# Accumulators of the backward gate's first block in the shared PSUM banks, and splits of attention values at the highest priority

## The chip, the cores and the metric

The kernel runs on one core of a Trainium2 chip. The metric is the device time of one execution in microseconds; lower is better. The kernel before takes 435.74 us, the median of three runs (435.19 to 435.88).

## The reference

One inference step of a hybrid diffusion backbone with one layer. 128 context tokens and 512 latent tokens (a grid of 8 rows of 64) of width 1024 go through the same weights. Each token is normalised, scaled and shifted by a modulation vector, and multiplied by one input projection of 1024 x 3840. Its columns feed three branches: neighbourhood attention with 8 heads of 64 (a query sees a window of 8 x 16 grid positions and 256 cached context keys), a gated linear recurrence in both directions with 4 heads and a 64 x 64 state each, and a Fourier transform over positions. Each branch is multiplied by a SiLU gate, and one output projection, a normalisation and a residual follow. Cut to what matters here:

```python
h = _rmsnorm(x, g_pre) * (1 + scale) + shift
proj = h @ w_in
qa, ka, va, ga, qr, zf, zb, ir, gr, uf, gf = _split_columns(proj)
...
lf_f, k_f = _hgrn_gates(zf, lb_f)      # forward gate of the recurrence
lf_b, k_b = _hgrn_gates(zb, lb_b)      # backward gate
...
s = jnp.concatenate([s_lat.reshape(B, H, GRID_W, kh * GRID_W), s_ctx], axis=-1)
p = jax.nn.softmax(s, axis=-1).astype(v.dtype)
v_all = jnp.concatenate([v_r.reshape(B, kh * GRID_W, H, dh), v_ctx], axis=1)
return jnp.einsum('bhqk,bkhd->bqhd', p, v_all)
```

## The kernel before

**Precision and splits.** Every operand of a large product is held as a high and a low part of a reduced format. `split` (L129 to L131) makes them: ScalarE casts the source to the high part (L130), VectorE subtracts it from the source to get the low part (L131). A product of two such operands is three matmuls (`mm3`, L210). All matmuls are recorded at the helper's line L113 and all transposes at L127; both run on TensorE.

**Blocks.** The input projection is cut into 30 blocks of 128 columns (the list `BLOCKS`). `block` (L299) loads one block's weights, splits them, and goes over the 640 tokens in two halves of 320 (u = 0 and 1). Each half is summed in one PSUM accumulator by 8 steps of three matmuls, 24 in all, and is then handed to a function that reads the accumulator. The modulated input, transposed, lies in `hT` as high and low part.

**PSUM banks.** There are eight banks. `PB(tag)` (L105) takes one from one of two pools by its tag: "b" has five banks, "f" has three (`WB`, L27). A bank that is asked for is waited for until the instructions that read its last contents are done. Pool "f" holds mostly the blocks' accumulators; pool "b" serves the start stage, the recurrence's levels and states, the attention's scores, transposes and sums.

**Start.** For each of the eight 128-row steps k of the input, `start_stream` (L244) computes the modulation, transposes the scaled input (`modulated`, L233, two "b" banks per step) and writes step k of `hT`. The forward gate's two blocks (zf0, zf1) are summed alongside in four accumulators, three of pool "f" and one of pool "b" (L208). When the last step is in, `gate` (L321) reads each with two sigmoids on ScalarE (L325, L326).

**Order of the work.** Generators for the start, the recurrences, the attentions and the blocks are interleaved by a small planner (`Order`, L39) with estimated costs and delays. The order in which it traces instructions is their priority. From it the program builder makes the final order of each engine's instructions: it simulates the engines, and on each one takes the ready instruction of the highest priority. A tile's buffer or bank is also given out in this simulation. `tc.high_priority()` puts the instructions traced inside it ahead of all others that are ready. On the chip each engine then works through its own list in order. `FILL` (L30) names the order of blocks: zb0 qr0 zb1 qr1 ir0 P0 P1 ga0 P2 and so on. zb0 is the backward gate's first block; P0 to P3 are the four attention pairs (two heads each).

**An attention pair.** `attention_blocks` (L574) runs block va (values), starts block qa (queries), and after two of its steps turns the values back to token order: `by_token` (L343) transposes the five blocks of 128 tokens, the first four into one "b" bank and the fifth into an "f" bank of its own. For each of the two heads three splits follow (L630 to L632): four token blocks from the "b" bank (128x256), one from the "f" bank (128x64), and the two blocks of cached values, which come from SBUF (`vcf`, tile `cf`). Their results lie in the tile `vs`. Then the cached keys are split, and blocks qa and ka go on. `attention` (L638) computes scores, softmax (L677 to L685), transposes of the probabilities and the weighted sums.

**The recurrence.** Each of its two parts goes through seven levels (L453 to L478) with six VectorE products, four ScalarE copies and masked copies out of PSUM (L451), then states (L504 to L528), whose recursion is L525, and outputs (L530 to L545).

Of the kernel before, what the change touches and what calls it, by code (L numbers as in the profile page):

```python
# [71 lines left out]
def mixer_kernel(ctx: ExitStack, tc: tile.TileContext, A, O):  # L72
# [14 lines left out]
    def nm(s):  # L87
        n_[0] += 1
        return f"{s}_{n_[0]}"

    def T(cols=NT, dt=F32, tag=""):
        return tp.tile([P, NT], dt, tag="t", name=nm("t" + tag))[:, :cols]
# [9 lines left out]
    def C():  # L102
        return sp.tile([P, 256], F32, tag="cf", name=nm("cf"), bufs=WB["cf"])

    def PB(tag="b"):  # L105
        return ps.tile([P, 512], F32, tag=tag, name=nm("pb"), bufs=WB["p" + tag])
# [22 lines left out]
    def split(src, hi, lo, hi_eng=None, lo_eng=None):  # L129
        (sc.copy if hi_eng is None else hi_eng.tensor_copy)(hi, src)  # L130
        (ve if lo_eng is None else lo_eng).tensor_sub(lo, src, hi.bitcast(F32))  # L131
# [16 lines left out]
    RS = [slice(0, 64), slice(64, 128)]  # L148
# [37 lines left out]
    def load_w(src, lo_eng=None, shape=(KT, P), tags=("raw", "hi", "lo")):  # L186

        return split_w(load_raw(src, tags[0], shape), lo_eng, shape, tags[1:])

    def load(t, src):  # L190

        with tc.issue_after(wdma[-1]) if wdma else ExitStack():
            sy.dma_start(t, src)
# [16 lines left out]
    def mm3(out, w, k, u, first, last):  # L210

        for a, (ww, hh) in enumerate(((w[0], 0), (w[0], 1), (w[1], 0))):
            mm(out, ww[:, k, :], hT[hh][:, k, 320 * u:320 * u + 320], start=(first and a == 0), stop=(last and a == 2))
# [85 lines left out]
    def block(name, use, lo_eng=ve):  # L299

        w = load_w(A["win"][BLOCKS.index(name)], lo_eng)
        for u in range(2):
            acc = PB("bf"[u] if name == "zb0" else "f")[:, 0:320]
            for k in range(KT):
                if name == "zb0" and u == 0 and f"h{k}" not in od.events:
                    yield f"h{k}"
                mm3(acc, w, k, u, k == 0, k == KT - 1)
                if k % 2 and k < KT - 1:
                    yield 0
            use(acc, u)  # L310
            if u == 1:
                od.set(f"block{nb[0]}", 0.0)
                nb[0] += 1
            yield 0
# [28 lines left out]
    def by_token(src):  # L343

        pt = PB(), PB("f")
        for i in range(5):
            tr(pt[i // 4][:, i % 4 * P:i % 4 * P + P], src[:, i * P:(i + 1) * P])
        return [(slice(4 * j, 4 + j), pt[j][:, 0:(4, 1)[j] * P].rearrange("p (i e) -> p i e", e=P)) for j in range(2)]
# [208 lines left out]
    def gate_block(name):  # L557
        j = GATE[name[:2]] + int(name[2])

        g = T(tag="g")  # L560

        def use(z, u):
            twice_silu(g[:, HF[u]], z)
            if u == 0:
                return
            if j in (4, 5):
                ve.tensor_scalar(g, g, late["ghg"][:, j - 4:j - 3], 0.5, op0=ALU.mult, op1=ALU.mult)
            mixed(j, gate=g)
        yield from block(name, use)
# [4 lines left out]
    def attention_blocks(p):  # L574
        tbl = sp.tile([P, 2, 2, 256], F32, tag="tbl", name=nm("tbl"), bufs=WB["tbl"])
        kf, kcf = T(tag="k"), C()
        vcf = C().rearrange("p (j e) -> p j e", e=P)
        load(kcf, A["kc"][p])
        load(vcf, A["vc"][:, :, p * P:(p + 1) * P])
        load(tbl, A["tbl"][p])  # L580
        vT, q = T(), T(tag="q")


        qs = [T(tag="qs", dt=F32R) for _ in range(2)]
        ks = [T(tag="ks", dt=F32R) for _ in range(2)]
        kcs = [sp.tile([P, 256], F32R, tag="kc", name=nm("kc"), bufs=WB["kc"]) for _ in range(2)]
        vs = tp.tile([P, 2, 7, P], F32R, tag="vs", name=nm("vs"), bufs=WB["vs"])
        att[p] = (tbl, qs, ks, kcs, vs)

        RW = slice(0, 3), slice(3, 8)  # L590

        def latent(z, u):
            return z[:, P * (1 - u):].rearrange("p (r c) -> p r c", c=64)

        def use_v(z, u):
            if u == 0:
                sc.copy(vT[:, 0:P], z[:, 0:P])
                sy.dma_start(O["o_v"][p], vT[:, 0:P])
            sc.copy(vT[:, P:NT].rearrange("p (j r c) -> p j r c", j=4, c=16)[:, :, RW[u], :],
                    latent(z, u).rearrange("p r (j c) -> p j r c", c=16))  # L600

        def use_q(z, u):
            if u == 0:
                sc.mul(q[:, 0:P], z[:, 0:P], 0.125)
            zl = latent(z, u)
            ql = q[:, P:NT].rearrange("p (q r c) -> p q r c", q=4, c=16)[:, :, RW[u], :]
            sc.mul(ql[:, 0:3], zl[:, :, 8:56].rearrange("p r (j c) -> p j r c", j=3), 0.125)
            sc.mul(ql[:, 3, :, 0:8], zl[:, :, 56:64], 0.125)
            sc.mul(ql[:, 3, :, 8:16], zl[:, :, 0:8], 0.125)
            if u == 0:  # L610
                return
            split(q, *qs, ve, QE)

        def use_k(z, u):
            if u == 0:
                ve.tensor_copy(kf[:, 0:P], z[:, 0:P])
                sy.dma_start(O["o_k"][p], kf[:, 0:P])
            ve.tensor_copy(kf[:, P:NT].rearrange("p (j r c) -> p j r c", j=4, c=16)[:, :, RW[u], :],
                           latent(z, u).rearrange("p r (j c) -> p j r c", c=16))
            if u == 0:  # L620
                return
            split(kf, *ks, ve, KE)
            od.set(f"a{p}", LAT["prep"])

        yield from block(f"va{p}", use_v)
        q_gen = block(f"qa{p}", use_q)
        yield next(q_gen)
        yield next(q_gen)
        vp = by_token(vT)
        for hh in range(2):  # L630
            for sl, src in vp + [(slice(5, 7), vcf)]:
                split(src[:, :, RS[hh]], vs[:, hh, sl, RS[hh]], vs[:, hh, sl, RS[1 - hh]])  # L632
        split(kcf, *kcs, ve, CE)
        yield 0
        yield from q_gen
        yield from block(f"ka{p}", use_k)
# [321 lines left out]
    def fill():  # L958
        yield "h4"
        for step in FILL.split():  # L960
            if step == "|":
                yield 0
                continue
            n, p = step[:2], int(step[-1])
            if n == "zb":
                yield from block(step, lambda z, u: gate(p, 1, z, u), ve)
            elif n == "qr":
                yield from block(step, lambda z, u: query(p, z, u), ve)
            elif n == "ir":
                yield from value_blocks()  # L970
            elif n[0] == "P":
                yield from attention_blocks(p)
            elif n[0] == "m":
                yield step
            elif n == "uf":
                yield from fourier_blocks()
            elif n == "F0":
                od.streams.insert(0, [fourier(), od.now])
            else:
                yield from gate_block(step)  # L980
        yield from out_first()
        yield from out_second()
# [148 lines left out]
```

## Time and profile before

| | before |
|---|---|
| median of three runs | 435.74 us |
| profiled execution | 436.31 us |
| its span, first to last instruction | 434.5 us |
| TensorE matmuls, busy | 410.3 us (94%) |
| TensorE weight loads, busy | 373.0 us (86%) |
| VectorE, busy | 303.2 us (70%) |
| ScalarE, busy | 204.7 us (47%) |
| DMA, mean of 16 engines | 110 GB/s |

PE is TensorE's matmul, PEld its weight load, which overlaps it, DVE VectorE, ACT ScalarE, POOL GpSimd and SP the engine that issues the DMAs. A row of a timeline gives start, duration, engine, line, operation, output and inputs, shape and count; in brackets stands how long the engine had idled before it, and what it had waited for. Where several like instructions follow each other, one row stands for all, with the time from the first start to the last end.

### The profile page before, as it was taken

How to read it: one execution, taken by the hardware profiler on the slowest of the kernel's cores; microseconds unless marked ns; L12 is line 12 of the kernel's file. 1: busy time of each engine (PE TensorE's matmuls, PEld its weight loads, DVE VectorE, ACT ScalarE, POOL GpSimd, SP SyncE). 2: the span in 40 equal slices, each digit the busy share in tenths (PEclk: the TensorE clock that was granted, in tenths of full speed). 3: DMA queues.
4: the chain of work that ended last, by engine and by line, in shares of the span. 5: the costliest groups of instructions: out<-in, count | busy, mean ns of one | idle time of the engine just before them, and what ended most of it. 6: DMA issues, size and time to landing. Idle time of an engine off the chain costs nothing.

```text
span 434.5 us, 8311 instructions
## 1 busy us (share of the span) xinstructions
PE 410.3 (94%) x3176; PEld 373.0 (86%) x3176; DVE 303.2 (70%) x866; ACT 204.7 (47%) x546; POOL 7.4 (2%) x23
## 2 busy tenths in 40 slices
PE   0699999999998999999999999999999999999994
PEld 0388899999988998999899989899898889988884
DVE  2775479999986865885597658786679748471164
ACT  5524467575341525654454534744456553251231
POOL 2000000000020100000000000000000000000000
PEclk9999999999999999999999999999999999999999
DMA  7996143211202011132112423245324203245032
GB/s 241 411 407 228 49 154 116 66 55 50 84 23 74 13 60 50 56 97 66 40 61 67 146 67 92 93 152 181 100 55 141 98 1 105 76 160 205 0 146 98
DMA packets 19528, 47.62 MB, mean 110 GB/s; under 512 B 3184, under 2 KB 6912, under 8 KB 19488
## 3 DMA queue, kind: packets, MB, share of 16 engines
q1 hardware_dynamic: 19376, 46.94, 31.7%
q8 instruction: 25, 0.41, 0.4%
q0 software_dynamic: 112, 0.14, 0.3%
q14 instruction: 15, 0.12, 0.1%
HBM read 43.80 MB, written 3.28 MB: 108 GB/s over the span
## 4 chain that ended last, share of the span: by engine, by line
PE 90%; DVE 4%; DMA 3%; ACT 1%; issue 1%; SPq 0%; DVEq 0%; ACTq 0%
PE pb L113 83%; PE pb L127 6%; DMA vs<-wss 1%; DMA txa<-x 1%; DVE AL L451 1%; DVE t L525 1%; DVE AL L488 0%; ACT L681 0%; DVE lo L131 0%; DVE t L953 0%; ACT hi L130 0%; ACT pe L682 0%; DVE t L468 0%; DVE t L467 0%; DVE AC L451 0%
## 5 line engine op out<-in xcount | busy, mean ns | idle before, releaser
L113 PE MATMUL pb<-hT,hi 128*128 128x320 f32 x896 | 209.5, 317 | 3.0 <-DVE vs L131 1.5
L113 PEld LDWEIGHTS pb<-hT,hi 128*128 128x128 f32 x896 | 149.4, 188 | 9.5 <-issue 2.3
L113 PE MATMUL pb<-hT,lo 128*128 128x320 f32 x448 | 139.0, 312 | 0.0
L113 PEld LDWEIGHTS pb<-hT,lo 128*128 128x128 f32 x448 | 84.1, 188 | 1.0 <-DVE G L274 0.2
L131 DVE TENSOR_TENSOR lo<-raw,hi 128x1024 fp32r<-128x1024 f32 x35 | 42.8, 1223 | 26.9 <-ACT hi L130 26.5
L130 ACT CAST hi<-raw 128x1024 fp32r<-128x1024 f32 x35 | 36.8, 1051 | 41.9 <-PE pb L113 20.9
L113 PE MATMUL pb<-t,t 64*128 64x128 f32 (+2 forms) x414 | 43.1, 291 | 0.4 <-DVE AL L451 0.4
L113 PEld LDWEIGHTS pb<-t,t 64*128 64x128 f32 (+1 forms) x414 | 36.2, 188 | 4.8 <-issue 0.8
L130 ACT CAST pT<-pb 128x256 fp32r<-128x256 f32 x64 | 23.3, 372 | 19.3 <-DVE pT L131 12.3
L113 PE MATMUL pb<-hi,mh 128*128 128x512 f32 (+1 forms) x108 | 32.1, 376 | 0.0
L131 DVE TENSOR_TENSOR pT<-pb,pT 128x256 fp32r<-128x256 f32 x64 | 26.4, 418 | 1.7 <-ACT pT L130 1.5
L113 PEld LDWEIGHTS pb<-hi,mh 128*128 128x128 f32 x108 | 19.4, 189 | 3.2
L113 PE MATMUL pb<-pT,mh 128*128 128x512 f32 (+1 forms) x102 | 22.2, 364 | 0.0
L681 ACT ACTIVATE pe<-pb,s 128x256 f32<-128x256 f32 x32 | 15.3, 477 | 13.8 <-DVE s L680 7.9
L127 PE MATMUL pb<-ident,pe 128*128 128x128 f32 x136 | 20.9, 273 | 0.5 <-ACT pe L682 0.5
L113 PEld LDWEIGHTS pb<-pT,mh 128*128 128x128 f32 x102 | 17.7, 189 | 3.1
L936 ACT ACTIVATE t<-pb 128x512 f32<-128x512 f32 (+1 forms) x11 | 6.0, 551 | 30.1 <-PE pb L113 30.1
L113 PE MATMUL pb<-lo,mh 128*128 128x512 f32 (+1 forms) x54 | 20.2, 373 | 0.0
L127 PEld LDWEIGHTS pb<-ident,pe 128*128 128x128 f32 x136 | 16.6, 140 | 1.4 <-ACT pe L682 0.7
L451 DVE COPY_PREDICATED AL<-masks,pb 128x512 f32<-128x512 uint32 x24 | 16.5, 738 | 1.5 <-PE pb L113 1.5
L113 PE MATMUL pb<-pT,vs 128*128 128x256 f32 (+1 forms) x96 | 16.8, 321 | 0.0
L113 PE MATMUL pb<-vs,csil 128*32 128x128 f32 x64 | 3.3, 335 | 14.3 <-DMA vs<-wss 14.3
(205 smaller groups left out, 636.3 us busy)
## 6 DMA issues: line engine op xcount, KB each, us to landing
raw<-win SPq DMA_DIRECT2D x30, 512.0 KB, 3.5
pT<-wss SPq DMA_DIRECT2D x12, 512.0 KB, 10.2
raw<-wg SPq DMA_DIRECT2D x8, 512.0 KB, 3.5
raw<-wout SPq DMA_DIRECT2D x8, 512.0 KB, 3.5
t<-x SPq DMA_DIRECT2D x10, 256.0 KB, 6.1
o_y<-t SPq DMA_DIRECT2D x9, 256.0 KB, 2.1
vs<-wss SPq DMA_DIRECT2D x4, 512.0 KB, 9.3
tbl<-tbl SPq DMA_DIRECT2D x4, 512.0 KB, 3.5
```

Source lines behind the costliest of these rows:

```text
L113: return te.matmul(out, lhsT, rhs, start=start, stop=stop).ins
L127: last_tr[0] = te.transpose(out, src, ident).ins
L130: (sc.copy if hi_eng is None else hi_eng.tensor_copy)(hi, src)
L131: (ve if lo_eng is None else lo_eng).tensor_sub(lo, src, hi.bitcast(F32))
L451: ve.copy_predicated(out, mk.to_broadcast([P, i1 - i0, P]), src)
L525: ve.scalar_tensor_tensor(sall[r, cdst], sall[r, cs], Td[r, ip:ip + 1], pst[r, cdst], op0=ALU.mult, op1=ALU.add)
L681: sc.activation(pe[:, 256:512], ss[:, 256:512], ACT.Exp, bias=m[:, 1:2], accum_out=m[:, 3:4])
L936: sc.activation(T(512)[:, cs], po[:, 0:cs.stop - cs.start], ACT.Square, accum_out=ssb[:, j:j + 1])
```

## The change

Two edits. The accumulator of zb0's second half is taken from pool "b", as that of its first half already is. And of an attention pair's value splits, those of the transposed tokens (two per head) are traced at the highest priority; the split of the cached values keeps its ordinary one and its place behind them.

```diff
-            acc = PB("bf"[u] if name == "zb0" else "f")[:, 0:320]
+            acc = PB("b" if name == "zb0" else "f")[:, 0:320]
...
         vp = by_token(vT)
         for hh in range(2):
-            for sl, src in vp + [(slice(5, 7), vcf)]:
-                split(src[:, :, RS[hh]], vs[:, hh, sl, RS[hh]], vs[:, hh, sl, RS[1 - hh]])
+            with tc.high_priority():
+                for sl, src in vp:
+                    split(src[:, :, RS[hh]], vs[:, hh, sl, RS[hh]], vs[:, hh, sl, RS[1 - hh]])
+            split(vcf[:, :, RS[hh]], vs[:, hh, 5:7, RS[hh]], vs[:, hh, 5:7, RS[1 - hh]])
         split(kcf, *kcs, ve, CE)
```

## The prediction

> **What bounds the kernel now.** I read the page first, then busy time by stage, then the waits of TensorE's queue, and last the order of time around the two places where TensorE stands still.
>
> ```profile
> span 434.5 us, 8311 instructions
> ...
> PE 410.3 (94%) x3176; PEld 373.0 (86%) x3176; DVE 303.2 (70%) x866; ACT 204.7 (47%) x546; POOL 7.4 (2%) x23
> ```
>
> ```profile
> 52.50:54.00 1.50, 0.48 (x4) 0.22 (x3) 0.00 (x0) 1.49 (x4) 0.00 (x0) 1.00 0.00 0
> 54.00:126.50 72.50, 72.14 (x633) 68.19 (x633) 66.85 (x153) 42.73 (x102) 2.42 (x6) 1.00 0.26 82
> 126.50:134.00 7.50, 6.02 (x48) 5.16 (x47) 6.99 (x27) 2.31 (x6) 0.00 (x0) 1.00 0.04 9
> 134.00:200.00 66.00, 65.53 (x496) 61.97 (x497) 48.10 (x147) 31.08 (x94) 1.91 (x6) 1.00 0.22 66
> 200.00:350.00 150.00, 149.55 (x1149) 136.75 (x1149) 108.88 (x362) 77.55 (x247) 0.00 (x0) 1.00 0.30 94
> 350.00:428.60 78.60, 78.57 (x426) 68.75 (x424) 40.26 (x79) 26.30 (x53) 0.00 (x0) 1.00 0.29 102
> ```
>
> The columns are the stretch, its length, then busy time of TensorE, its weight loads, VectorE, ScalarE and GpSimd, the granted clock (1.00 throughout) and DMA. TensorE is the bound: from 134 to 428.6 it idles 0.47 + 0.45 + 0.03 = 0.95 us in all. Only two stretches stand out, with 1.50 - 0.48 = 1.02 us and 7.50 - 6.02 = 1.48 us idle. The second half is full of work, so an idle microsecond of TensorE that is taken out early can reach the end, if nothing else holds back the work that moves up. VectorE could: it is 93% busy from 126.5 to 134 (6.99 of 7.50) and 92% in the stretch before (66.85 of 72.50).
>
> ```profile
> PE pb L113 <- DVE vs L131: 1.5, 1, 1.5
> PE pb L113 <- ACT t L326: 1.0, 1, 1.0
> PE pb L127 <- ACT pe L682: 0.5, 1, 0.5
> ```
>
> These are TensorE's longest waits once data is there. The first is for a VectorE subtraction that belongs to an attention pair's values, the second for a sigmoid of the forward gate. They are the two places that the diff touches. The third is for a softmax.
>
> **Accumulators of the first backward block.**
>
> ```profile
> 42.35 1.04 ACT L130 CAST hi<-raw 128x1024 fp32r<-128x1024 f32 x1
> ...
> 42.90 0.76 PE L127 MATMUL pb<-ident,txb 128*128 128x128 f32 x5
> ...
> 49.16 0.46 ACT L239 ACTIVATE t<-pb,shift,G 128x128 f32<-128x128 f32 x1 [0.99 <-PE pb L127]
> ...
> 51.70 1.28 ACT L325 ACT_TABLE_LOAD   x1 [2.08 <-PE pb L113]
> ...
> 52.34 0.31 PE L113 MATMUL pb<-hT,hi 128*128 128x320 f32 x1
> ...
> 52.49 0.31 PE L113 MATMUL pb<-hT,lo 128*128 128x320 f32 x1
> 53.00 0.44 ACT L325 ACTIVATE t<-pb 128x320 f32<-128x320 f32 x1
> 53.33 0.43 ACT L326 ACTIVATE t<-pb 128x320 f32<-128x320 f32 x1
> 53.65 1.05 ACT L130 CAST hi<-raw 128x1024 fp32r<-128x1024 f32 x1
> ...
> 54.73 1.23 DVE L131 TENSOR_TENSOR lo<-raw,hi 128x1024 fp32r<-128x1024 f32 x1 [3.72 <-ACT hi L130]
> ```
>
> ```profile
> 53.81 0.41 PE L113 MATMUL pb<-hT,hi 128*128 128x320 f32 x1 [1.02 <-ACT t L326]
> ```
>
> The second half of zb0 asks for one of three "f" banks, and all three hold sums of the forward gate. The first comes free when both sigmoids (L325, L326) have read it, and the table load stands ahead of them. Matmuls follow one another every 0.15 us (52.34 to 52.49), so the gap from 52.49 to 53.81 costs 1.32 - 0.15 = 1.17 us. With a "b" bank this half needs nothing from ScalarE. Of five "b" banks one holds the forward gate's fourth sum and one zb0's first half; the last that the start stage uses is read by 49.16 + 0.46 = 49.62. So one is free at 52.6 and taking it costs nothing. Nor can the half take it too early, ahead of the start stage's last wide transposes: its weights were cast from 42.35 to 43.39, and those transposes began at 42.90.
>
> What is late next is qr0's weights. The half is 24 matmuls, 24 x 0.147 = 3.5 us, so TensorE wants qr0 at 52.64 + 3.53 = 56.2. The high part is ready at 53.65 + 1.05 = 54.7, the low part at 54.73 + 1.23 = 55.96: a margin of 0.2 us. If the cast falls behind one more pair of sigmoids (0.44 + 0.43), 0.7 us is lost again; behind two, all of it. The term lies between 0 and -1.17. I take -1.17, because the cast's place does not depend on the bank.
>
> The Trainium skill, "ScalarE: Activation LUTs", section "What ACT_TABLE_LOAD costs", gives a switch of tables 1.28 us for the load and 1.38 for a drain. The trace shows the load alone: 1.30 us from 51.70 to the sigmoid at 53.00, on an engine that had idled before. By the page's sum this stall, and so this term, would be 1.38 us larger, 2.55; the measured row decides.
>
> **Splits of the values by token.**
>
> ```profile
> 127.03 0.21 ACT L130 CAST vs<-pb 128x64 fp32r<-128x64 f32 x1
> ...
> 130.79 0.23 DVE L131 TENSOR_TENSOR vs<-pb,vs 128x64 fp32r<-128x64 f32 x1
> ...
> 131.06 0.21 ACT L130 CAST vs<-pb 128x64 fp32r<-128x64 f32 x1 [3.24 <-DVE vs L131]
> ...
> 132.07 0.31 PE L113 MATMUL pb<-hT,lo 128*128 128x320 f32 x1
> ...
> 133.50 0.21 DVE L131 TENSOR_TENSOR vs<-pb,vs 128x64 fp32r<-128x64 f32 x1
> 133.74 0.91 DVE L525 SCALAR_TENSOR_TENSOR t<-t,m,pb 64x64 f32<-64x64 f32 x3
> ```
>
> ```profile
> 133.86 0.38 PE L113 MATMUL pb<-hT,hi 128*128 128x320 f32 x1 [1.48 <-DVE vs L131]
> ```
>
> The last of five transposed blocks has an "f" bank of its own. Its first cast is done at 127.24, but VectorE runs recurrence work first and subtracts at 130.79; ScalarE's second cast waits 3.24 us for that, and the last subtraction ends at 133.71. Then the next accumulator gets the bank. TensorE's loss is 133.86 - 132.07 - 0.15 = 1.64 us. At the highest priority the three steps behind the first cast follow one another with at most one running instruction (some 0.5 us) ahead of each: 3 x (0.5 + 0.22) = 2.2, so the bank is free by 129.4, well before TensorE asks at 132.2. No split or DMA is added; only ScalarE's and VectorE's orders change, and the cached values' splits keep their place. Recurrence work slips by two subtractions, 0.44 us, and regains it where they used to stand. The term lies between 0 and -1.64. I take -1.64.
>
> **What is given back.** TensorE then comes to the recurrence 1.17 + 1.64 = 2.81 us sooner. VectorE's chain need not.
>
> ```profile
> 66.25 0.29 DVE L130 CAST kc<-cf 128x256 fp32r<-128x256 f32 x1 [2.88 <-DMA cf<-kc]
> ...
> 120.41 1.34 DVE L451 COPY_PREDICATED AL<-masks,pb 128x512 f32<-128x512 uint32 x2 [1.48 <-PE pb L113]
> ```
>
> ```profile
> 137.32 0.55 PE L113 MATMUL pb<-t,AL 128*128 128x64 f32 x4
> ```
>
> Between these two VectorE rows no other VectorE wait is listed; the first is for a DMA, so the unbroken stretch starts where it did. The recurrence's states are done at 133.74 + 0.91 = 134.65, and TensorE begins to use them at 137.32. That is 2.67 us of slack; the shift of 2.81 exceeds it by 0.14, which is lost again. I add +0.14. Were the slack nothing, both terms would be lost.
>
> In pairs 1 to 3 the splits now stand ahead of softmax work.
>
> ```profile
> L131 DVE TENSOR_TENSOR vs<-pb,vs 128x256 fp32r<-128x256 f32 x8 | 3.3, 414 | 0.5 <-ACT vs L130 0.4
> ...
> L130 ACT CAST vs<-pb 128x256 fp32r<-128x256 f32 x8 | 3.1, 386 | 6.7 <-DVE vs L131 3.4 <-PE pb L127 3.3
> ...
> L131 DVE TENSOR_TENSOR vs<-pb,vs 128x64 fp32r<-128x64 f32 x8 | 1.7, 217 | 0.0
> ...
> L130 ACT CAST vs<-pb 128x64 fp32r<-128x64 f32 x8 | 1.7, 215 | 3.3 <-DVE vs L131 3.2
> ```
>
> One pair's splits are 2 x (0.414 + 0.386 + 0.217 + 0.215) = 2.46 us as a relay, because the engines wait for each other on one bank (3.4 and 3.2 us of such waits). Three pairs: 7.4 us. TensorE's cost lies between 0 (it has other blocks' matmuls to run) and 7.4. The nearest row is its one softmax wait, 0.5; I take +0.3.
>
> The order of TensorE's instructions changes as well, since the program is ordered anew. Its small idles bound that.
>
> ```profile
> PEld pb L113 <- issue: 9.9, 43, 1.7
> ```
>
> Without the longest these are 8.2 us in 42 places, 0.2 each; five more or fewer give 1.0 either way. I take 0.
>
> The sum: -1.17 - 1.64 + 0.14 + 0.3 = -2.37. The profiled execution took 436.31 us (434.5 and 1.81 around it), so 433.94; the median of the three timed runs is 0.57 lower than the profiled one, so 433.4.
>
> **Rivals.** *VectorE takes it all back.* If its chain through the recurrence, and not TensorE, sets when the stage up to 146 ends, both gains turn into waits inside it: 435.7. For it speak the 92 and 93%; against it the 2.67 us of slack, and that VectorE itself waits 1.48 us for TensorE at 120.41. The change not doing what it says belongs here: the splits could stay where they are if they were held by data and not by order. The cast done at 127.24 and used at 130.79 speaks against that.
>
> *Only one stall goes.* Either qr0's cast falls behind sigmoids, which leaves the second term, 435.74 - 1.64 + 0.3 = 434.4, or the states' slack absorbs the second, which leaves the first, 435.74 - 1.17 + 0.3 = 434.9.
>
> *The relay hits the softmax: slower.* With the splits ahead of a pair's exponentials, TensorE's transposes of the probabilities come late in pairs 1 to 3. Half of 7.4 is 3.7: 435.74 - 2.81 + 0.14 + 3.7 = 436.8; all of it 440.5. It eats the gain from 2.67 of 7.4 (36%), and is slower by over 0.2% from 48%. Against it: TensorE idles 0.95 us in 295 behind 134, so other work is nearly always at hand. For it: the one softmax wait, 0.47 us, lies beside pair 1's splits.
>
> ```profile
> 172.99 0.47 ACT L130 CAST vs<-pb 128x256 fp32r<-128x256 f32 x2
> ...
> 173.20 0.63 PE L127 MATMUL pb<-ident,pe 128*128 128x128 f32 x4 [0.47 <-ACT pe L682]
> ```
>
> The Trainium skill, "PSUM — Partial Sum Buffer", section "PSUM bank collisions raise a hardware error", says that ScalarE and VectorE must not read one bank at once; the waits between the halves agree. By that rule no priority makes the relay shorter than its sum.
>
> **How the numbers follow.** Forecast 0.54, with a range of its own from 432.5 to 434.6; one stall alone 0.15; all given back 0.15; relay 0.16. About 0.2%, 0.87 us, is what a measurement can tell from no change, so faster means under 434.87: the forecast and most of the one-stall case, 0.67. Same: 0.16. Slower: 0.17. The range goes up to 436.8, the half relay, and down to 432.3: both terms in full (-2.81) and three idles of 0.2 fewer. Outside remain the worse half of the relay and a luckier order.
>
> **What would show it.** Right: no wait of TensorE for L326 and the gate's sigmoids after zb0's second half has begun; no wait of 1.5 us for the values' subtraction; casts and subtractions of 128x64 within 2.5 us of the transpose; an idle sum behind the start about 2.5 us lower. Wrong: a wait for qr0's low part near 56; TensorE idle between 132 and 147 on VectorE or on a bank that a late evacuation holds; a sum of softmax waits above 2 us.

## The result, and the profile after

The changed kernel takes 437.64 us (median of seven runs, 436.63 to 438.83); the kernel before, in the same comparison, 435.30. The ratio is 1.0054, with a 95% interval from 1.0043 to 1.0066: slower by 0.54%, about 2.3 us, where 433.4 was forecast, a gain of 2.3.

The head of the page of the changed kernel:

```profile
span 435.7 us, 8312 instructions
...
PE 411.7 (94%) x3176; PEld 373.6 (86%) x3176; DVE 303.3 (70%) x866; ACT 204.7 (47%) x546; POOL 7.4 (2%) x23
```

The work is the same (3176 matmuls, 866 VectorE instructions); only its order and its waits differ. TensorE's waits in the changed kernel, behind the one for the first weights, longest first (total, times, longest):

```profile
PE pb L113 <- DVE vs L131: 1.3, 1, 1.3
PE pb L113 <- ACT hi L130: 1.2, 1, 1.2
PE pb L127 <- ACT pe L684: 0.5, 1, 0.5
```

The wait for the sigmoid (L326, 1.0) is gone. In its place stands one of 1.2 us for the high part of a block's weights. The wait for the values' subtraction, which the second edit was to remove, went from 1.5 to 1.3. The softmax wait is as it was.

The two profiled executions did not start alike: step 7 of `hT` was written 0.9 us earlier in the changed kernel. To compare them, take the start of the last subtraction of the start stage (L241) and the start of the last matmul. Before:

```profile
50.18 0.83 DVE L241 TENSOR_TENSOR hT<-t,hT 128x640 fp32r<-128x640 f32 x1
...
428.29 0.28 PE L113 MATMUL pb<-lo,mh 128*128 128x256 f32 x1
```

After, with the rows around the first place of the change:

```profile
49.27 0.83 DVE L241 TENSOR_TENSOR hT<-t,hT 128x640 fp32r<-128x640 f32 x1
...
53.57 1.28 ACT L325 ACT_TABLE_LOAD   x1 [4.86 <-PE pb L113]
...
54.86 0.44 ACT L325 ACTIVATE t<-pb 128x320 f32<-128x320 f32 x1
55.09 0.31 PE L113 MATMUL pb<-hT,lo 128*128 128x320 f32 x1
...
55.52 1.05 ACT L130 CAST hi<-raw 128x1024 fp32r<-128x1024 f32 x1
...
56.61 1.23 PE L113 MATMUL pb<-hT,hi 128*128 128x320 f32 x4 [1.22 <-ACT hi L130]
...
57.88 0.42 PE L113 MATMUL pb<-hT,lo 128*128 128x320 f32 x1
...
62.57 1.05 ACT L130 CAST hi<-raw 128x1024 fp32r<-128x1024 f32 x1 [1.77 <-DMA raw<-win]
...
429.48 0.28 PE L113 MATMUL pb<-lo,mh 128*128 128x256 f32 x1
```

From `hT` to the last matmul are 428.29 - 50.18 = 378.11 us before and 429.48 - 49.27 = 380.21 after: 2.10 us more, close to the 2.3 of the timed runs. I call this stretch the tail; it leaves the start stage's variation out. In every run 2760 matmuls start behind the L241 row, so the place of a matmul in this count can be compared between runs as well.

The cause is at the top of that fence. ScalarE waits for the first of the forward gate's sums for 4.86 us, where it waited for 2.08. In the order of TensorE's instructions, 19 of the 24 matmuls of zb0's second half now stand ahead of the last matmul of the forward gate. Of them 18, those of steps 0 to 5, stand ahead of all of the gate's step 7, which they don't need: 18 x 0.147 = 2.65 us. The nineteenth stands ahead of the last matmul of the sum that is read first, which makes 2.79 us. The trace agrees: 29 matmuls start between the L241 row and the table load, where 10 did before. Against the L241 row, the table load comes at 53.57 - 49.27 = 4.30, before at 51.70 - 50.18 = 1.52: 2.78 us later. The two sigmoids behind it and qr0's cast (55.52) are as much later, and TensorE, done with zb0, waits for qr0: first 1.22 us for the high part (56.61), then until 57.88 for the low part. The 45th matmul of the tail, the one at 57.88, starts 8.60 us behind the L241 row; before, the 45th starts 7.84 us behind it. So up to here the new wait costs 0.76 us more than the one that is gone; the rest of the 2.1 is lost later.

Why could the half come first? In the kernel before, all three "f" banks held sums of the forward gate until a sigmoid had read one. The wait for the bank was also the only thing that kept the second half behind the gate. With a "b" bank at hand the program builder, which puts the first ready instruction into TensorE's list, had 18 ready matmuls to put there.

The second place, in the changed kernel:

```profile
128.41 0.21 ACT L130 CAST vs<-pb 128x64 fp32r<-128x64 f32 x1
...
132.07 0.23 DVE L131 TENSOR_TENSOR vs<-pb,vs 128x64 fp32r<-128x64 f32 x1
...
132.33 0.21 ACT L130 CAST vs<-pb 128x64 fp32r<-128x64 f32 x1 [3.13 <-DVE vs L131]
...
134.66 0.23 DVE L131 TENSOR_TENSOR vs<-pb,vs 128x64 fp32r<-128x64 f32 x1
...
135.03 0.53 PE L113 MATMUL pb<-hT,hi 128*128 128x320 f32 x2 [1.26 <-DVE vs L131]
```

Almost nothing moved: between the first cast and its subtraction still lie 3.4 us (3.55 before), and ScalarE still waits 3.13 us (3.24 before). In VectorE's order the first subtraction passed one instruction (L476), and the second one more (an L525).

### The profile page after: what moved, and what is told of

It reads as the page before. It is cut to its first block, busy times and chain, and to the rows that moved or that the text cites. A ratio compares the mean times of both kernels' runs of the same rounds, so it can differ in the third digit from the quotient of the medians.

```text
span 435.7 us, 8312 instructions
## 1 busy us (share of the span) xinstructions
PE 411.7 (94%) x3176; PEld 373.6 (86%) x3176; DVE 303.3 (70%) x866; ACT 204.7 (47%) x546; POOL 7.4 (2%) x23
## 4 chain that ended last, share of the span: by engine, by line
PE 90%; DVE 4%; DMA 3%; ACT 2%; issue 1%; SPq 0%; DVEq 0%; ACTq 0%
PE pb L113 83%; PE pb L127 6%; DMA vs<-wss 2%; DMA txa<-x 1%; DVE AL L451 1%; DVE t L525 1%; ACT hi L130 0%; DVE AL L488 0%; ACT L683 0%; DVE lo L131 0%; DVE t L955 0%; ACT pe L684 0%; DVE t L468 0%; DVE t L467 0%; DVE AC L451 0%
## 5 line engine op out<-in xcount | busy, mean ns | idle before, releaser
L113 PE MATMUL pb<-t,t 64*128 64x128 f32 (+2 forms) x414 | 44.3, 292 | 0.4 <-DVE AL L451 0.4
L113 PEld LDWEIGHTS pb<-t,t 64*128 64x128 f32 (+1 forms) x414 | 37.1, 188 | 5.1 <-DVE AL L451 0.9
L451 DVE COPY_PREDICATED AL<-masks,pb 128x512 f32<-128x512 uint32 x24 | 16.6, 743 | 0.6 <-PE pb L113 0.6
```

The source lines that it names most:

```text
L113: return te.matmul(out, lhsT, rhs, start=start, stop=stop).ins
L451: ve.copy_predicated(out, mk.to_broadcast([P, i1 - i0, P]), src)
```

## The experiments

Theory A: the bank edit alone carries the loss, because the half runs ahead of the gate, and the priority edit does next to nothing. Rival B: the splits' new priority disturbs VectorE and costs the time. A second question, if A holds: is the wait of 1.17 us worth anything when the order is kept? A1 says that TensorE sets the pace and it is; A2 says that VectorE's chain behind qr0's cast sets the pace and it isn't.

The results, against runs of the kernel before on the same chip (its medians were 435.31, 435.52, 435.32 and 435.27 in the four comparisons):

| run | median us | ratio, 95% interval | tail us |
|---|---|---|---|
| before | 435.3 | | 378.11 |
| changed kernel | 437.64 | 1.0054 (1.0043 to 1.0066) | 380.21 |
| bank edit alone | 438.08 | 1.0057 (1.0037 to 1.0076) | 380.72 |
| priority edit alone | 435.19 | 0.9988 (0.9977 to 0.9999) | 377.94 |
| bank edit, held | 435.52 | 1.0002 (0.9991 to 1.0014) | 378.48 |
| table at the start | 434.60 | 0.9972 (0.9958 to 0.9985) | 376.83 |
| split first, by order | 434.66 | 0.9977 (0.9967 to 0.9987) | 376.96 |
| third buffer | 435.59 | 1.0000 (0.9990 to 1.0010) | 378.10 |
| held, third buffer | 434.10 | 0.9969 (0.9957 to 0.9980) | 376.83 |
| held, table, third buffer | 434.39 | 0.9969 (0.9957 to 0.9980) | 376.82 |
| held, 20 transposes ahead | 434.05 | 0.9973 (0.9962 to 0.9983) | 377.01 |
| changed, third buffer | 436.96 | 1.0045 (1.0029 to 1.0060) | 380.96 |
| changed, table | 436.38 | 1.0026 (1.0013 to 1.0038) | 379.56 |
| held, third buffer, split first | 433.06 | 0.9957 (0.9943 to 0.9972) | 375.72 |
| changed, 26 transposes ahead | 437.49 | 1.0041 (1.0026 to 1.0056) | 380.25 |
| changed, table, third buffer | 435.52 | 0.9998 (0.9990 to 1.0007) | 378.11 |
| changed, held | 435.85 | 1.0010 (0.9999 to 1.0021) | 378.26 |

**The two edits apart.** First the accumulator's bank alone, then the splits' priority alone. The f-piece is the fifth block of values, the one in an "f" bank of its own.

> The bank edit alone: the backward gate's first block in the two shared banks, no split at highest priority. Theory A (the free bank lets the second half's matmuls run ahead of the forward gate's last step, so the gate's sigmoids and qr0's cast come about 1.9 us later and everything behind them on VectorE with it): about 2.3 us slower than the kernel before, 437.3 to 437.9, with the sigmoids of line 325 ending near 54.9 instead of 53.0. Rival B (the loss comes from the splits' new priority): 434.0 to 435.3, no slower than before.

> The priority edit alone: splits of the value pieces at highest priority, the first block's halves in the banks of the kernel before. Theory A: no change, 434.8 to 435.8, since the f-piece's split keeps 12 or more VectorE instructions in front of it and TensorE's wait for it near 133 us stays. Rival B (the loss comes from here): 436.5 or more.

The bank edit alone is slower by 0.57%, the priority edit alone faster by 0.12%, 0.5 us, at the edge of its interval (by medians it is 0.1 us). In the run of the bank edit, 0.2 us above what I had named, the first sigmoid starts at 55.04 and qr0's wait of 1.22 us is there. B falls, and A holds as to the edit; how much of the loss goes through the sigmoids these two runs don't show.

**The bank without the order.** The second half's matmuls are issued behind the gate's last one, so that every engine's order is that of the kernel before. The traces confirm it: the rows of TensorE, VectorE and ScalarE follow one another in the same order in both.

```diff
+        gate_mm.append(last_mm[0])
...
-            acc = PB("bf"[u] if name == "zb0" else "f")[:, 0:320]
+            acc = PB("b" if name == "zb0" else "f")[:, 0:320]
...
-                mm3(acc, w, k, u, k == 0, k == KT - 1)
+                with tc.issue_after(gate_mm[0]) if name == "zb0" and u == 1 else ExitStack():
+                    mm3(acc, w, k, u, k == 0, k == KT - 1)
```

> The bank edit, with the second half's matmuls held behind the last matmul of the forward gate, so that every engine has the order of the kernel before and only the bank differs: TensorE's wait for qr0's low part (1.17 us before) goes, and no sigmoid is late. Theory A1 (TensorE sets the pace of the early stage): the gain that was forecast for this edit, 434.1. Theory A2 (VectorE's chain that starts at qr0's cast sets the pace, and TensorE only waits elsewhere): 435.3, no change; the time removed near 53 us comes back as a wait before 150 us. Rival B, where the bank itself costs something (a later eviction of the shared bank): 436 or more.

The loss is gone, so it came from the order. But the gain did not come either: A2 named the time. The wait at 52.5 is away, and two others appeared. From the held run's timeline (L455 is L451 of before, the masked copy out of a level's bank):

```profile
60.01 1.05 ACT L130 CAST hi<-raw 128x1024 fp32r<-128x1024 f32 x1 [2.26 <-DMA raw<-win]
...
81.87 1.24 PE L113 MATMUL pb<-t,t 64*128 64x128 f32 x16 [0.16 <-DVE AL L455]
...
83.61 0.49 PE L113 MATMUL pb<-t,t 64*128 64x128 f32 x2 [0.50 <-DVE AC L455]
```

TensorE comes about 1.2 us sooner to the level's products and waits there for VectorE's copies, which are no sooner. By the count of matmuls the 185th of the tail still starts 1.28 us earlier than before (25.67 against 26.95 us behind the L241 row), the 285th 0.21 us later (38.49 against 38.28): the gain is lost between the two, 0.66 us of it in the two waits shown. Measured from the L241 row, the cast of qr1's weights (60.01) is late: 60.01 - 48.99 = 11.02, where before it is 59.87 - 50.18 = 9.69. That cast waits for a load. The load was issued on the release of qr0's raw buffer, as early as before; it took longer. The time from issue to landing of that one load in the kernel before:

```profile
DMA to landing us min/median/max: 3.8/3.8/3.8
```

and in the held run:

```profile
DMA to landing us min/median/max: 5.1/5.1/5.1
```

Why? The DMA view of the held run from 55 to 58 us, where that load moves, shows a second queue beside it; before, the same window (55 to 58) has none, and the fetch comes at 59.3, half a microsecond before that load is done:

```profile
q1 hardware_dynamic: 136, 0.50, 47.4%
q8 instruction: 1, 0.02, 1.9%
```

The whole kernel has 25 such packets of 16 KB. From the page of the kernel before:

```profile
q8 instruction: 25, 0.41, 0.4%
```

TensorE has 2 x 3176 = 6352 matmuls and weight loads, 254 for each of the 25. So this is TensorE's code, and it moves with TensorE: the held run, 1.17 us ahead, brought the fetch into the load. The records of the packets show one such packet of 0.93 us, and of the load's 16 parts fifteen done by 58.29 and the last at 59.93. In the changed kernel it is alike, with a fetch at 60.47: fifteen parts by 61.18, the last at 62.49. Call this theory L: the term is real, and the fetch took it away. The Trainium skill, "Runtime: NRT & Kernel Launch", section "Instruction fetch mechanics", says that an engine's sequencer refills its code in 16 KiB blocks over a DMA queue of its own, at a cost that is mostly hidden; the packets agree with the first (16 KB each), and the held run with its fetch moved, below, shows that this one was not hidden (0.29%).

**The table out of the way.** One sigmoid of a constant tile ahead of the start stage, TensorE's and VectorE's orders as before:

```diff
         scale_x()
+        sc.activation(cp.tile([P, 1], F32, tag="warm", name="warm"), rstd[:, 4:5], ACT.Sigmoid)
```

> The kernel before, with one small sigmoid of a constant tile at the start, so that the sigmoid table is loaded before the gate needs it; TensorE's and VectorE's orders are those before. It takes about 1.28 us of table load out of the way to qr0's cast, with both bank waits as before. If the time follows qr0's cast (A, and A2 above all): 434.0 to 434.4. If it doesn't (the chain has slack at qr0, or TensorE has): 435.3.

It is 0.28% faster (434.60 us, 0.2 above the range I had named), and the tail is shorter by 378.11 - 376.83 = 1.28, the table load's own time. From its timeline:

```profile
50.65 0.44 ACT L326 ACTIVATE t<-pb 128x320 f32<-128x320 f32 x1 [2.10 <-PE pb L113]
...
51.30 1.05 ACT L130 CAST hi<-raw 128x1024 fp32r<-128x1024 f32 x1
```

The sigmoids start as soon as the sum is there, the bank is free before TensorE asks, and the weights' chain is earlier as well. Here TensorE and the loads moved together, so it doesn't tell A1 from A2 by itself.

**The load out of the way.** zb1's raw weights go to a buffer that the start stage has left, so the loads behind start one release earlier. TensorE's order is that before.

```diff
-        w = load_w(A["win"][BLOCKS.index(name)], lo_eng)
+        w = load_w(A["win"][BLOCKS.index(name)], lo_eng, tags=("pT" if name == "zb1" else "raw", "hi", "lo"))
```

> The kernel before, with zb1's raw weights loaded into one of the buffers that the start stage has left, so that the three weight loads behind it, and the loads of pair 0's cached keys that follow them in the queue, start one release earlier. TensorE's order is that before, VectorE's differs in 6 lines. If the loads that start on the release of qr0's raw buffer set when VectorE's unbroken stretch begins (66.25 before), and VectorE the pace up to 134: the stretch begins 1.5 to 3 us earlier, TensorE's wait near 132 shrinks or goes, 433.5 to 434.5. If TensorE sets the pace of the stage: 435.3 within 0.4, and VectorE only idles elsewhere.

> The same buffer for zb1's raw weights, with the bank edit and the second half held behind the forward gate as in the run before: the bank wait of 1.17 us is gone and nothing else of TensorE's order changes. Theory L (in the held run the 1.17 us was eaten because a 16 KB fetch of code, which moves with TensorE, fell into the load of qr1's weights, whose last sixteenth came 1.6 us late, 5.2 us from issue to cast where it was 3.9): with the load out of the way the term comes through, 0.9 to 1.2 us faster than the run with the third buffer alone. Theory A2 (VectorE's work itself leaves TensorE no slack between 66 and 134): the same time as that run within 0.3, with new waits of TensorE for VectorE of about 1 us near 82.

> All three: third buffer, the bank edit held behind the forward gate, and the sigmoid table loaded at the start. If no chain through qr0's cast is left once the loads have a third buffer: within 0.3 of the held run with the third buffer. If qr0's cast still leads VectorE's chain: 0.8 to 1.2 us below it. Either way the fastest of the eight so far, 432.0 to 433.5.

The buffer alone is worth nothing (1.0000), although VectorE's unbroken stretch begins 1.9 us sooner (63.32 - 49.13 = 14.19 against 66.25 - 50.18 = 16.07): TensorE's wait near 132 stays 1.5 us. So VectorE was not what set the pace, and my guess for this run was wrong. With the held bank edit on top, 0.31% come through: the tail is 1.27 us shorter than with the buffer alone, and no wait near 82 is left. That is A1 and the forecast's first term, and A2 falls. The table adds nothing more; the run with all three, which I had put at 432.0 to 433.5, missed by 0.9 us.

**The fetch out of the way.** To move the fetches (all of them come some 20 matmuls earlier) and no order, TensorE does 20 unused transposes at its start, where it waits for the first weights anyway.

```diff
+    pad = PB()
+    for _ in range(20):
+        te.transpose(pad[:, 0:P], ident, ident)
```

> The held run again (the bank edit, the second half behind the forward gate), with 20 transposes of the identity at TensorE's start, where it waits 14 us for the first weights. They compute nothing that is used. TensorE fetches its code in blocks of 16 KB, about every 250 of its instructions, so 40 more instructions bring the fetch that began at 56.8 forward by 20 matmuls of 0.147 us, to about 53.9, ahead of the load of qr1's weights. Theory L: that load's last sixteenth comes with the others, its cast 3.7 to 4.0 us after its issue (5.2 in the held run), TensorE's waits near 82 go, and the time is 434.0 to 434.4. Rival (the load was late for another reason, or the 1.17 us are eaten by VectorE): 435.3 to 435.7, as the held run.

The fetch now comes at 52.7. The load takes, from issue to landing:

```profile
DMA to landing us min/median/max: 3.5/3.5/3.5
```

and qr1's cast waits 0.67 us for it instead of 2.26:

```profile
58.97 1.05 ACT L130 CAST hi<-raw 128x1024 fp32r<-128x1024 f32 x1 [0.67 <-DMA raw<-win]
```

The held run gains what it lacked: 0.27% faster than before, tail 377.01 against 378.48, the cast 58.97 - 55.34 = 3.63 us after the issue. Twenty transposes that nobody uses are worth 0.29% (1.0002 to 0.9973), some 1.3 us, by moving the fetch. L holds for the held run. The same transposes in the kernel before were not tried.

**The split really first.** Instead of a priority, an order: pair 0's state instructions on VectorE (L512, L525) come behind the f-piece's last subtraction.

```diff
+                if p == 0 and hh == 1 and sl == slice(4, 5):
+                    for ins in states:
+                        tc.add_manual_dep(ins, last_sub[0].ins.name, ...
```

> The kernel before, with pair 0's f-piece split really put first: VectorE's copies and steps of the same recurrence's states are ordered behind the last of the two subtractions, so that these move up by 9 and 13 places in VectorE's order (in the changed kernel the first moved up by one). It is the priority edit as the prediction took it. The prediction's second term: TensorE's wait of 1.5 us near 132 goes or falls below 0.3, and the kernel takes 433.7 to 434.3. Rival (VectorE sets the pace of this stage, and the displaced states or level products make TensorE wait behind it): the wait near 132 goes, 1.0 us or more of new waits appear before 150, and the time stays at 434.9 to 435.5.

From its timeline (L132 and L133 are the split's two lines):

```profile
127.13 0.21 ACT L132 CAST vs<-pb 128x64 fp32r<-128x64 f32 x1
...
128.42 0.22 DVE L133 TENSOR_TENSOR vs<-pb,vs 128x64 fp32r<-128x64 f32 x1
...
128.67 0.21 ACT L132 CAST vs<-pb 128x64 fp32r<-128x64 f32 x1 [0.76 <-DVE vs L133]
...
129.43 0.22 DVE L133 TENSOR_TENSOR vs<-pb,vs 128x64 fp32r<-128x64 f32 x1
```

The four steps take 129.65 - 127.13 = 2.5 us instead of 6.7, the bank is free 2.5 us before TensorE asks, and TensorE no longer idles there. The window from 128 to 135.2, first of the kernel before, then of this run (length, TensorE's busy time and matmuls first):

```profile
128.00:135.20 7.20, 5.72 (x44) 4.86 (x44) 6.64 (x23) 1.26 (x2) 0.00 (x0) 1.00 0.05 11
```

```profile
128.00:135.20 7.20, 7.20 (x55) 6.38 (x54) 6.79 (x26) 1.26 (x2) 0.00 (x0) 1.00 0.05 11
```

Of 1.48 us idle nothing is left; the tail is 1.15 us shorter and the time 0.23% lower, 1.0 us. It missed what I expected (433.7 to 434.3) by 0.4, since 0.3 us is lost again. Where isn't visible as idle time of TensorE. Its own order changed too, in places from its 1131st to its 1384th matmul, so this run doesn't move the split alone.

**Both waits removed.** The held bank edit, the third buffer, and this order together.

> The bank edit held behind the forward gate, the third buffer for the raw weights, and pair 0's f-piece split put first by order: both waits of TensorE that the change was aimed at are removed. If the two terms add (1.3 and 1.0 us in the runs of each alone): 433.0 to 433.4, the fastest of all. If both were the same slack: 434.1.

433.06 us, 0.43% faster than before: the terms add, and nothing of the two waits is left in its list:

```profile
PE pb L113 <- DVE hT L244: 1.4, 1, 1.4
PE pb L127 <- ACT pe L696: 0.5, 1, 0.5
PE pb L113 <- DVE t L133: 0.4, 1, 0.4
```

The first of these lies in the start stage. The tail lost 378.11 - 375.72 = 2.39 us, of the 2.81 that the forecast's two terms promised.

**What the changed kernel's loss is made of.** Four runs with the changed kernel: the third buffer, the table, both, and a pad that moves the code fetch.

> The changed kernel, with zb1's raw weights in a buffer that the start stage has left, so that the load that a code fetch delays in it (4.7 us from issue to cast) starts earlier. If the late load is a part of the loss of 2.3 us: 0.6 to 1.0 us faster than the changed kernel, 436.5 to 437.0; the rest is TensorE's wait for qr0's weights near 56. If the loss is all in that wait and in the late sigmoids: 437.4 to 437.9.

> The changed kernel, with the sigmoid table loaded at the start. The second half still runs ahead of the forward gate's last step, but the sigmoids, and qr0's cast behind them, come 1.28 us sooner than in the changed kernel. If the loss runs through qr0's cast: TensorE's wait near 56 shrinks from 1.2 to about 0, and the time is 435.9 to 436.6. If it is the half's place in TensorE's order itself that costs: 437.3 or more.

> The changed kernel with 26 transposes of the identity at TensorE's start, whose results are not used; every order behind them is the changed kernel's. The code fetch that began at 60.5 moves forward by 26 matmuls, ahead of the load of qr1's weights. If the late load is a share of the loss: that load's cast comes 3.7 to 4.0 us after its issue (4.7 before), and the kernel is 0.7 to 1.2 us faster than the changed kernel, 436.4 to 436.9. If the loss is the late sigmoids alone: 437.4 to 437.9.

> The changed kernel with the table loaded at the start and zb1's raw weights in the third buffer. If the late sigmoids (1.28 us of them are the table's) and the late load (0.7 to 1.2) are the whole loss: 435.0 to 435.7, level with the kernel before. If either was only a shift of the wait to another place: 436.2 or more.

The table takes 1.26 us of the 2.3 away by medians (437.64 - 436.38); the profiled execution, the slowest of its nine, shows 0.65 of it. With the third buffer on top the kernel is level with the kernel before, in time and in tail (378.11 both). Level is not undone, though: the table alone is worth as much in the kernel before (0.28% in both), and with the half held, table and buffer give 434.39 us and a tail of 376.82. Against that run the half's place still costs 1.29 us of tail and 0.29%. From the timeline of the changed kernel with both:

```profile
53.31 0.44 ACT L326 ACTIVATE t<-pb 128x320 f32<-128x320 f32 x1 [4.87 <-PE pb L113]
...
55.08 1.22 PE L113 MATMUL pb<-hT,hi 128*128 128x320 f32 x4
...
56.34 0.41 PE L113 MATMUL pb<-hT,lo 128*128 128x320 f32 x1
```

The sigmoid starts 53.31 - 49.00 = 4.31 us behind the subtraction of `hT`, 2.77 us later than with the half held (50.42 - 48.88), and TensorE's first four matmuls on qr0 take 1.26 us, not 4 x 0.147 = 0.59, before the low part is there. So the late sigmoids and qr0's cast are a part of the loss, and these runs don't show that they and the loads are all of it. With the table alone a wait is seen as in the held run: the load takes 5.2 us, and TensorE waits for a level's copy:

```profile
84.44 1.81 PE L113 MATMUL pb<-t,t 64*128 64x128 f32 x18 [0.30 <-DVE AL L452]
```

Where the rest is lost can be counted. In the changed kernel the 185th matmul of the tail starts 0.86 us later than before, the 385th 2.19 (50.72 against 48.53 us behind the L241 row), and behind that no more than 0.1 us is lost. So 1.33 us go between these two, in a stretch where the held run and the bank edit alone lose 1.7 each. In the held run that was the fetch; in the changed kernel it is not settled. The third buffer alone gave 0.7 us by medians and the pad 0.15, with intervals that overlap each other and the changed kernel's. With the pad the load was in time (3.5 us) and the tail no shorter (380.25), so taking the fetch out of the load gains nothing there. In the third buffer's profiled execution the granted clock was 0.81 in one stage:

```profile
57.00:66.00 9.00, 8.97 (x51) 8.86 (x51) 6.98 (x13) 5.15 (x11) 0.00 (x0) 0.81 0.51 161
```

In it the 60 matmuls from the 45th to the 105th took 10.44 us, where they take 8.90 in the changed kernel. Without these 1.54 us the tail would be 379.42, 0.8 shorter than the changed kernel's. But the buffer does two things here: loads start sooner, and TensorE's order, which differs from that before also between its 570th and 979th matmul (28 rows), is nearly put back there (8 rows). Which of the two gives the 0.8 us, no run tells apart.

**The changed kernel with only the hold.**

> The changed kernel with the second half held behind the forward gate's last matmul, both edits otherwise as they are. The sum of the two edits' own runs (held bank edit 0.0, priority edit -0.5): 434.6 to 435.5, and with the code fetch in the load as in the held run, waits of TensorE of about 1 us near 82. If the loss came from the two edits together: 436.5 or more.

435.85 us, ratio 1.0010: no longer slower by anything that this measurement tells, and 0.35 above what I expected. The wait for a level's copy (0.5 us, AC L455) is there, as in the held run. With the half held, the change is worth nothing here: the fetch eats its first term, as in the held run, and of its second next to nothing was there.

## Why the prediction was wrong

*What bounds the kernel.* Right. TensorE sets the pace through both places: 2.39 us of its two waits reach the end when they are removed and the load is kept clear of the fetch, and VectorE's 92 and 93% busy time was no bound (the third buffer made VectorE's stretch start 1.9 us sooner for nothing).

*The accumulators: the step that failed.* The size was right: -1.17 forecast, 1.28 of tail with the order held and the load clear. What failed is "I take -1.17, because the cast's place does not depend on the bank", and with it "Nor can the half take it too early, ahead of the start stage's last wide transposes". The cast's place among ScalarE's instructions indeed stayed. But it stands behind two sigmoids, these stand behind the gate's last matmuls, and those now stand behind 19 matmuls of the half, 2.8 us. I looked at what the half could delay by taking a bank (the transposes) and not at what it could delay by taking TensorE. The two sigmoids' rows and the 24 matmuls were all in the text.

*Where TensorE's order would change.* I bounded this by small idles, 1.0 us either way, and took 0. The bound looked at how often TensorE waits briefly, not at what the removed wait had been keeping in place. The bank edit alone came out at +2.5 us (0.57%) with its own wait removed; against the held run, which differs from it in the order alone, the order cost 2.6 us by medians and 2.2 by tail. By the 45th matmul of the tail, where TensorE has waited for qr0's weights, 2.04 of these are lost (8.60 us against 6.56 in the held run). That is the step that failed, measured in one place.

*What is late next.* The margin at qr0's weights, 0.2 us, and the sign given for a wrong forecast ("a wait for qr0's low part near 56") were to the point: the wait came at 56.6. I had priced it at 1.17, the whole term, as if the stall could only come back and never grow.

*The splits.* -1.64 forecast; 0.5 us by time and 0.17 by tail in the priority edit's own run. Seven tenths of it (by tail nine) failed at "at the highest priority the three steps behind the first cast follow one another". Priority chooses among instructions that are ready in the builder's simulation; VectorE's list changed by one place there, so in the simulation the split had hardly been behind anything. On the chip VectorE gets to it 3.4 us late, and a priority can't repair that. This reading of the builder is argued from the order lists, not tried. That the split can be moved, and then pays 1.0 us, was shown with an explicit order.

*Given back, and the relay.* +0.14 forecast; with both waits removed, 2.81 - 2.39 = 0.42. The relay's +0.3 did not come: the softmax wait is 0.5 us before and after, so the slower rival that I had priced at 436.8 played no part. The rival that did happen, a half that delays the gate, was not on my list, and 437.64 lies 0.84 above the range.

*The table load.* The trace's 1.30 us was the right price and the larger sum of 2.55 was not: without the load the tail is 1.28 us shorter.

## What to carry to other kernels

A wait for a buffer is also an order: before you remove it, list every instruction that becomes ready without it, and ask what stands behind them on the same engine. If the work behind is on the way to other engines, keep the order by an explicit edge and remove only the wait. A remedy that makes a slow version level again proves little until the fast version has had it too. And a high priority is no promise of a place: look at the order that results.

## What the runs showed of the hardware

TensorE's code comes in packets of 16 KB, 25 for its 6352 matmuls and weight loads, about one for every 254, and the profile counts the packets' time on the 16 DMA engines that carry the data too. When such a packet (0.93 us) fell into a 512 KB load of the held run, 15 of the load's 16 parts landed on time and one 1.6 us later; the load took 5.1 us instead of 3.8. Moving the fetch by 20 unused transposes took the load to 3.5 us and the kernel's time down by some 1.3 us. In the changed kernel 26 transposes took the load from 4.6 to 3.5 us, and the tail did not change (380.21 and 380.25): a late load need not cost time.
